# One load cut into 2 and 6 rows in a rotary-embedding kernel that streams 67 MB

## Chip, cores, metric

The kernel runs on one core of one Trainium2 chip. (The experiments used three chips; each was compared with the kernel before in the same rounds on the same chip.) The metric is the time of one execution on the device in microseconds (us). Other times below are counted from the start of the profiled span, which is some 2 us shorter than the device time of the same run.

## The reference, cut to what matters

```
x: (16, 512, 16, 64) float32;  cos, sin: (512, 32) float32
x1, x2 = x[..., :32], x[..., 32:]
first  = x1[..., :16] * cos[..., :16] - x1[..., 16:] * sin[..., :16]
second = x1[..., :16] * sin[..., :16] + x1[..., 16:] * cos[..., :16]
out = concatenate([first, second, x2], axis=-1)
```

Half of each head is rotated, the other half is copied. All of x, 33.6 MB, is read and the same amount is written.

## The kernel before

The kernel cuts x into four tiles of 128 partitions x 16 rows; one row is 16 heads x 64 numbers, 4 KiB. A tile is 8.4 MB, and the kernel keeps room for three, so tile 3 takes the place of tile 0. VectorE rotates a tile in place, in pieces of 8 rows (tile 2's second half in 5 and 3). Loads of x, and all stores but that of tile 2, are issued in program order by SyncE.

```
    def load(t, lo=0, hi=K):
        return nc.sync.dma_start(out=rows(t, lo, hi), in_=xf[t, :, lo * R : hi * R])
    ...
    load(0)
    load(1)
    load(2, 0, KC)                       # KC = 8 rows
    ...                                  # tables of cos and sin
    rotate(0, 0, KC)
    rotate(0, KC, K)
    store(0)
    load(2, KC, K)                       # the load that is changed
    load(3)                              # waits for store(0): same place in memory
    rotate(1, 0, KC)
    rotate(1, KC, K)
    behind_loads = store(1)              # made to wait for `near`
    rotate(2, 0, KC)
    near = rotate(2, KC, KM)             # KM = 13
    rotate(2, KM, K)
    store(2, queue=nc.gpsimd)
    ...
    rotate(3, 0, KC)
    rotate(3, KC, K)
    store(3)
```

Of the kernel before, what the change touches and what calls it, by code (L numbers as in the profile page):

```python
# [1 line left out]

# [4 lines left out]


@with_exitstack
def kernel(  # L10
    ctx: ExitStack,
    tc: tile.TileContext,
    x: bass.AP,
    cos: bass.AP,
    sin: bass.AP,
    out: bass.AP,
):
    nc = tc.nc
    fp32 = mybir.dt.float32
    P = 128  # L20
    B, S, H, D = x.shape
    Q = D // 4
    HF = D // 2



    K = 16
    T = B * S // (P * K)
    PB = S // K
    REP = P // PB  # L30
    R = H * D
    NS = 3
    KC = K // 2
    KM = 13

    xf = x.rearrange("b s h d -> (b s h d)").rearrange("(t p f) -> t p f", t=T, p=P)
    of = out.rearrange("b s h d -> (b s h d)").rearrange("(t p f) -> t p f", t=T, p=P)
    cosf = cos.rearrange("(p k) j -> p (k j)", k=K)
    sinf = sin.rearrange("(p k) j -> p (k j)", k=K)

    const_pool = ctx.enter_context(tc.tile_pool(name="const", bufs=1))
    b_pool = ctx.enter_context(tc.tile_pool(name="bp", bufs=1, space=bass.MemoryType.PSUM))


    ring = const_pool.tile([P, NS, K, H, D], fp32)
    stage = const_pool.tile([P, 2, K, HF], fp32)
    spun = const_pool.tile([P, 2 * K, Q], fp32)
    packed = const_pool.tile([PB, 2 * K, Q], fp32)
    table = const_pool.tile([P, 2, K, 2, Q], fp32)

    def rows(t, lo, hi):
        return ring[:, t % NS, lo:hi].rearrange("p k h d -> p (k h d)")

    def load(t, lo=0, hi=K):
        return nc.sync.dma_start(out=rows(t, lo, hi), in_=xf[t, :, lo * R : hi * R])

    def store(t, lo=0, hi=K, queue=nc.sync):
        return queue.dma_start(out=of[t, :, lo * R : hi * R], in_=rows(t, lo, hi))  # L58


    nc.vector.memset(stage[:, :, :, 0:Q], 0.0)  # L61
    spread = stage.rearrange("(j b) t k i -> j b t (k i)", b=REP)
    nc.gpsimd.dma_start(out=spread[:, 0, 0], in_=cosf)  # L63
    nc.gpsimd.dma_start(out=spread[:, 0, 1], in_=sinf)  # L64
    load(0)
    load(1)
    load(2, 0, KC)




    PQ = PB // REP
    nc.vector.stream_shuffle(  # L73
        out=spun[:],
        in_=stage.rearrange("p t k j -> p (t k) j")[:, :, 0:Q],
        mask=[j % PQ * REP for j in range(PB)],
    )
    for q in reversed(range(REP)):
        n = PQ * (q + 1)
        nc.vector.tensor_copy(out=packed[0:n], in_=spun[q * PB : q * PB + n])  # L80

    for r in range(REP):
        nc.vector.tensor_copy(  # L83
            out=table[r * PB : (r + 1) * PB].rearrange("p t k c j -> p (t k) c j"),
            in_=packed.unsqueeze(2).to_broadcast((PB, 2 * K, 2, Q)),
        )
    C = table[:, 0].rearrange("p k c j -> p k (c j)")
    Sn = table[:, 1].rearrange("p k c j -> p k (c j)")

    def rotate(t, lo, hi):  # L90
        x1 = ring[:, t % NS, lo:hi, :, 0:HF]
        c = C[:, lo:hi].unsqueeze(2).to_broadcast((P, hi - lo, H, HF))
        s = Sn[:, lo:hi].unsqueeze(2).to_broadcast((P, hi - lo, H, HF))
        b_full = b_pool.tile([P, KC, H, HF], fp32, name="b_t")
        b_t = b_full[:, 0 : hi - lo]
        nc.vector.tensor_mul(out=b_t, in0=x1, in1=s)  # L96
        nc.vector.tensor_mul(out=x1, in0=x1, in1=c)  # L97
        nc.vector.tensor_sub(  # L98
            out=x1[:, :, :, 0:Q], in0=x1[:, :, :, 0:Q], in1=b_t[:, :, :, Q:HF]
        )  # L100
        return nc.vector.tensor_add(  # L101
            out=x1[:, :, :, Q:HF], in0=x1[:, :, :, Q:HF], in1=b_t[:, :, :, 0:Q]
        )

    rotate(0, 0, KC)
    rotate(0, KC, K)
    store(0)
    load(2, KC, K)
    load(3)
    rotate(1, 0, KC)  # L110
    rotate(1, KC, K)
    behind_loads = store(1)
    rotate(2, 0, KC)
    near = rotate(2, KC, KM)
    rotate(2, KM, K)
    store(2, queue=nc.gpsimd)

    tc.add_manual_dep(
        behind_loads.ins,
        near.ins.name,  # L120
        mybir.DependencyInfo(mybir.DependencyClass.Sync, mybir.DependencyReason.DATA),
        reason="the store follows the loads at the DMA engines",
# [6 lines that stand above are left out]
# [1 line left out]
_INS = ['x', 'cos', 'sin']  # L130
_OUTS = [((16, 512, 16, 64), 'float32')]


# [23 lines left out]
```

## Time and profile before

| | before |
|---|---|
| time, median of 3 runs | 161.46 us |
| profiled span | 159.5 us |
| VectorE busy | 112.9 us (71%) |
| both DMA queues, share of 16 engines | 98.1% |
| DMA packets | 1360, of them 1152 on the hardware queue |
| last landing of a transfer to the end of the span | 0.886 us |

The lines of the profile are shown in the prediction.

### The profile page before, as it was taken

The numbers are of one execution on the slowest core, as the hardware profiler recorded it, in microseconds if no ns is written. First come the engines' busy times: TensorE is split into PE (matmuls) and PEld (weight loads), VectorE is DVE, ScalarE is ACT, GpSimd is POOL, SyncE is SP. The second block draws the span as 40 slices with busy tenths as digits, with TensorE's granted clock in tenths as the row PEclk, the third lists the DMA queues.
The fourth block names the chain that finished last, engine by engine and source line by source line (L and its number), as shares of the span: only waits on it lengthen the run. The fifth ranks groups of instructions, "written<-read, shape, count | busy, mean of one in ns | idle before, by whom it ended". The sixth has DMA issues, their size and how long they took to land.

```text
span 159.5 us, 115 instructions
## 1 busy us (share of the span) xinstructions
DVE 112.9 (71%) x47; POOL 1.9 (1%) x7
## 2 busy tenths in 40 slices
DVE  1000959999999999999999999999999990000000
POOL 3000000000000000000000000010000000000000
DMA  7969979899699699699996996996996996998966
GB/s 263 542 263 542 444 345 526 362 427 526 271 493 551 263 526 526 263 395 427 493 526 263 526 526 263 526 526 263 526 526 263 526 510 279 526 427 362 526 263 263
DMA packets 1360, 67.24 MB, mean 422 GB/s; under 512 B 176, under 2 KB 176, under 8 KB 208
## 3 DMA queue, kind: packets, MB, share of 16 engines
q1 hardware_dynamic: 1152, 58.72, 85.7%
q0 software_dynamic: 208, 8.52, 12.4%
HBM read 33.69 MB, written 33.55 MB: 422 GB/s over the span
## 4 chain that ended last, share of the span: by engine, by line
DVE 61%; DMA 14%; issue 5%; DVEq 1%
DVE b_t L96 22%; DVE ring L97 22%; DMA ring<-in_x_dram 14%; DVE ring L101 10%; DVE ring L98 7%; DVEq L152 1%; DVEq L96 0%
## 5 line engine op out<-in xcount | busy, mean ns | idle before, releaser
L96 DVE TENSOR_TENSOR b_t<-ring,table 128x4096 f32<-128x4096 f32 (+2 forms) x9 | 35.6, 3959 | 2.1 <-DMA ring<-in_x_dram 1.9
L97 DVE TENSOR_TENSOR ring<-ring,table 128x4096 f32<-128x4096 f32 (+2 forms) x9 | 35.6, 3950 | 0.3
L98 DVE TENSOR_TENSOR ring<-ring,b_t 128x2048 f32<-128x2048 f32 (+2 forms) x9 | 18.4, 2050 | 0.3
L101 DVE TENSOR_TENSOR ring<-ring,b_t 128x2048 f32<-128x2048 f32 (+2 forms) x9 | 18.4, 2043 | 0.0
L73 DVE LOAD_MASK_SELECT spun<-stage x1 | 0.0, 14 | 14.4 <-DMA stage<-in_sin_dram 14.4
L83 DVE COPY table<-packed 32x1024 f32<-32x1024 f32 x4 | 2.7, 684 | 0.1
L58 POOL DMA_DIRECT2D out_dram<-ring x1 | 0.6, 559 | 101.7 <-DVE ring L101 101.7
L80 DVE COPY packed<-spun 32x512 f32<-32x512 f32 (+3 forms) x4 | 1.7, 416 | 0.1
L61 DVE MEMSET stage<- 128x512 f32 x1 | 0.5, 485 | 0.9 <-PEq L141 0.9
L73 DVE STREAM_SHUFFLE spun<-stage 128x512 f32<-128x512 f32 x1 | 0.7, 722 | 0.0
L63 POOL DMA_DIRECT2D stage<-in_cos_dram x1 | 0.6, 642 | 1.3 <-DVE stage L61 1.3
L64 POOL DMA_DIRECT2D stage<-in_sin_dram x1 | 0.5, 532 | 0.0
L141 POOL MEMSET const-bfloat16-1.0<- 128x1 bf16 x1 | 0.1, 101 | 0.0
L141 POOL MEMSET const-float32-0.0<- 128x1 f32 x1 | 0.1, 98 | 0.2 <-issue 0.2
L141 POOL MEMSET const-float32-1.0<- 128x1 f32 x1 | 0.1, 98 | 0.0
L141 POOL MEMSET const-uint8-127<- 128x1 uint8 x1 | 0.1, 98 | 0.0
## 6 DMA issues: line engine op xcount, KB each, us to landing
ring<-in_x_dram SPq DMA_DIRECT2D x2, 4096.0 KB, 40.7
stage<-in_cos_dram POOLq DMA_DIRECT2D x1, 64.0 KB, 8.9
stage<-in_sin_dram POOLq DMA_DIRECT2D x1, 64.0 KB, 13.3
ring<-in_x_dram SPq DMA_DIRECT2D x3, 28.9
out_dram<-ring SPq DMA_DIRECT2D x3, 27.4
out_dram<-ring POOLq DMA_DIRECT2D x1, 39.5
```

The costliest lines, as they stand in the source:

```text
L58: return queue.dma_start(out=of[t, :, lo * R : hi * R], in_=rows(t, lo, hi))
L61: nc.vector.memset(stage[:, :, :, 0:Q], 0.0)
L63: nc.gpsimd.dma_start(out=spread[:, 0, 0], in_=cosf)
L64: nc.gpsimd.dma_start(out=spread[:, 0, 1], in_=sinf)
L73: nc.vector.stream_shuffle(out=spun[:], in_=stage.rearrange("p t k j -> p (t k) j")[:, :, 0:Q], mask=[j % PQ * REP for j in range(PB)],)
L80: nc.vector.tensor_copy(out=packed[0:n], in_=spun[q * PB : q * PB + n])
L83: nc.vector.tensor_copy(out=table[r * PB : (r + 1) * PB].rearrange("p t k c j -> p (t k) c j"), in_=packed.unsqueeze(2).to_broadcast((PB, ...
L96: nc.vector.tensor_mul(out=b_t, in0=x1, in1=s)
L97: nc.vector.tensor_mul(out=x1, in0=x1, in1=c)
L98: nc.vector.tensor_sub(out=x1[:, :, :, 0:Q], in0=x1[:, :, :, 0:Q], in1=b_t[:, :, :, Q:HF])
L101: return nc.vector.tensor_add(out=x1[:, :, :, Q:HF], in0=x1[:, :, :, Q:HF], in1=b_t[:, :, :, 0:Q])
L152: with _tile.TileContext(nc) as tc:
```

## The change

Its likely intent is to have a small first piece of the half tile arrive early, or small packets first where the transfers turn from a store to a load. The whole of it:

```
@@ rotate(0, KC, K); store(0) @@
-    load(2, KC, K)
+    load(2, KC, KC + 2)
+    load(2, KC + 2, K)
     load(3)
```

## The prediction

> **What bounds the kernel now.** I read the page first, then the chain of waits, the SyncE queue's own waits, the timeline, the stretches by window, and last the packet records of the trace (one row per DMA packet: queue, size, start, duration). The page:
>
> ```profile
> span 159.5 us, 115 instructions
> ## 1 busy us (share of the span) xinstructions
> DVE 112.9 (71%) x47; POOL 1.9 (1%) x7
> ...
> ## 3 DMA queue, kind: packets, MB, share of 16 engines
> q1 hardware_dynamic: 1152, 58.72, 85.7%
> q0 software_dynamic: 208, 8.52, 12.4%
> HBM read 33.69 MB, written 33.55 MB: 422 GB/s over the span
> ## 4 chain that ended last, share of the span: by engine, by line
> DVE 61%; DMA 14%; issue 5%; DVEq 1%
> ```
>
> The reader is to see two candidates. The chain names VectorE (61%), but VectorE is busy for 71% of the span, while the packets of the two DMA queues take 85.7 + 12.4 = 98.1% of the time of all 16 engines. The chain is followed through semaphores and so does not see a transfer that queues behind another. The SyncE queue's waits show that queueing:
>
> ```profile
> SPq L152 <- DMA out_dram<-ring: 26.8, 2, 14.4
> SPq L58 <- DMA ring<-in_x_dram: 22.3, 2, 20.8
> SPq L55 <- DMA out_dram<-ring: 21.0, 1, 21.0
> ```
>
> After VectorE's last instruction there are still 26.8 us of waiting for stores. One 8.4 MB tile is 8 packets of 64 KiB on each engine; the packet records give 2418 ns for such a packet and 2414 ns from start to start, so alone it would take 8 x 2.414 = 19.3 us. The other 7 us are a backlog of older stores: VectorE has finished early, and the transfers set the end. The stretches say the same, with the share of the 16 engines next to last and GB/s last:
>
> ```profile
> 2.00:50.00 48.00, 31.94 (x19) 0.87 (x2) 1.00 0.96 415
> 50.00:100.00 50.00, 49.59 (x17) 0.00 (x0) 1.00 1.02 438
> 100.00:158.00 58.00, 30.89 (x12) 0.56 (x1) 1.00 0.98 424
> ```
>
> (A packet is booked where it starts, hence 1.02.) When I string the packets of each engine together, every engine works from 1.7-2.2 us to 158.0-158.2 us, and the largest hole inside that, before the last 0.3 us, is 9 ns. So the kernel is bound by bytes: 67.24 MB through 16 DMA engines that never run dry. Outside this stretch lie 1.7 us until the first packet and about 1.3 us from the last packet to the end.
>
> Two places could open a hole, where loads run out and a store takes over. The timeline:
>
> ```profile
> 49.87 0.35 SPq L58 DMA_DIRECT2D out_dram<-ring  x1
> ...
> 50.26 21.82 SPq L55 DMA_DIRECT2D ring<-in_x_dram  x2
> ...
> 98.86 32.68 SPq L58 DMA_DIRECT2D out_dram<-ring  x2
> ```
>
> The first load was issued at 0.74 and its first packet started at 1.74, so an issue needs 1.0 us to reach the engines. The store of tile 0, issued at 49.87, could start at 50.87; the loads ahead of it drained at about 51.25: 0.4 us to spare. The store of tile 1, issued at 98.86, could start at 99.86; its first packet started at 99.855, as the first engine finished its loads: nothing to spare. The kernel is tuned tightly there.
>
> **What the Trainium skill says.** "Perfetto Trace Analysis", Roofline, says that one core alone is bounded by its 16 DMA engines, about 435 GB/s together. The trace agrees: 65,536 bytes in 2.414 us times 16 is 434 GB/s in steady state. "DMA: Bandwidth & Descriptors", Bandwidth, gives the rule to batch transfers to 1 MiB or more and says that smaller ones pay mostly overhead; one of the two pieces here is just 1 MiB (128 x 8 KiB). But its figure for that size, 341 GB/s, is for a transfer with nothing around it. Here the table loads' 4 KiB packets, interleaved with x's, took 159 ns, and 4/64 of 2418 would be 151: inside a full queue a small packet costs nanoseconds. The same page, Queues, rings and completion order, says that each engine takes its ring's descriptors in order; the trace agrees, since the second half of tile 2 starts only when tile 0's store has ended on its engine. So a piece placed behind that store cannot arrive earlier by being smaller.
>
> **The change part by part.** One SyncE load of rows 8-15 of tile 2 (128 packets of 32 KiB) becomes a load of rows 8-9 (128 of 8 KiB) and one of rows 10-15 (128 of 24 KiB). The order of instructions on VectorE and GpSimd is unchanged; SyncE has one more DMA; the product of rows 8-12 now waits on two load semaphores and not on one. Bytes, tiles and the order of loads and stores stay.
>
> Packets: each engine moves 8 partitions, so it gets 8 more data packets and one more semaphore packet. A split packet's cost can be read from sizes present: a 64 KiB packet takes 2414 ns from start to start, a 32 KiB one 1209.5; two of the latter, 2419, are 4.7 ns more. So 8 x 4.7 + 1 x 6 (the semaphore packet's step) = 44 ns per engine. It lies on the bound, so it counts in full: **+0.04 us**.
>
> Issue: one more SyncE issue of 0.33-0.43 us (the five load issues range from 328 to 433 ns). SyncE next has to issue the load of tile 3, which waits for tile 0's store until 71.8: 21.0 us of waiting by the table above. The extra 0.4 us goes into it: **0**.
>
> Earlier data: rows 8-9 would land about 6 us ahead of the rest (three quarters of 8 x 1.21 = 9.7 us), near 75 us. Their reader needs rows 8-12, so both pieces, and VectorE does not get to it before 90.22, while the whole half landed at 81.34 (last of its 16 semaphore increments). There are 8.9 us of slack already: **0**.
>
> End: the final row of semaphore waits gets one member more, about 0.03 us as a guess from the 21-28 ns of such events in the trace: **+0.03**.
>
> The loads then end 0.04 us later, so the store of tile 1, issued when VectorE says so at 98.86, finds the engines still busy; that gap doesn't open. Sum: +0.07 us on 161.46, thus **161.5 us**.
>
> **Rivals.**
>
> 1. The turn from stores to loads gets cheaper. On 14 of 16 engines the last packet of tile 0's store is not 2418 ns but 2432-3318 ns, and all engines end it between 70.85 and 71.25; this excess averages 0.37 us per engine. Small first packets after a store are perhaps there to fill that. For it: this is the only place in mid-kernel where packets are slow, and it is right before the load that the change cuts. Against it: the slow packet is the store's, which the change leaves alone, and a gain is capped, since the store of tile 1 cannot start before 99.86 and now starts between 99.86 and 100.26; 0.2 us on average would be kept, giving 161.3.
>
> 2. Small packets are slow after all. If an engine can have only few reads in flight, 8 KiB packets could run at half speed: 1 MiB at 434 GB/s is 2.4 us, so up to +2.4 us, 163.9. Against it are the 4 KiB packets at 159 ns; for it, that these alternated with 64 KiB ones and were never eight in a row.
>
> 3. VectorE becomes the bound through a late second piece. It would have to land 8.9 us later than now. The packet sum gives 0.04 us, so I don't believe it.
>
> 4. The extra issue holds up the tile 3 load. At its issue, tile 2's half is still ahead of it (it drains until about 80.8), so even a delay of 8 us would be hidden.
>
> **Range and chances.** The centre is 161.5. The runs before spread from 161.22 to 161.59, and rival 1 takes at most some tenths; rival 2, which I give one chance in ten in some weakened form, puts a tail above. The range is 161.0 to 162.1. 2% is 3.2 us: faster would need fewer bytes or a hole that isn't there (0.01), slower needs more than the worst of rival 2, or one I don't see (0.02).
>
> **What would show it.** Right: 1296 packets on the hardware queue in place of 1152 (128 data and 16 semaphore packets more), still about 98% of the engines; no hole in any engine; the product of rows 8-12 again at about 90.2 with no wait for a load; the store of tile 1 issued at about 98.9. The packets: 8 KiB near 306 ns, 24 KiB near 911 ns (2414 per 64 KiB, plus 5). Wrong: 8 KiB packets of 500 ns or more (rival 2); tile 0's last store packets all at 2418 ns (rival 1); idle time on VectorE ahead of rows 8-12 (rival 3). The number would be wrong without any of these if the chip's runs scatter by more than the three I have.

## The result, and the profile after

In its first six runs the changed kernel took 161.94 us (161.80 to 161.99), the kernel before 161.44 us in its six runs (161.22 to 161.62). The ratio was 1.0029, with a 95% interval of 1.0016 to 1.0042. (A ratio is the mean time of one kernel's fast runs over that of the other's of the same rounds, so it is not quite the ratio of the medians quoted beside it.) That is within 2% and within the stated range, but +0.5 us where the working said +0.07 us.

The first lines are from the page of the changed kernel, packets and queues:

```profile
span 159.9 us, 117 instructions
...
DMA packets 1504, 67.24 MB, mean 421 GB/s; under 512 B 192, under 2 KB 192, under 8 KB 224
## 3 DMA queue, kind: packets, MB, share of 16 engines
q1 hardware_dynamic: 1296, 58.72, 85.7%
q0 software_dynamic: 208, 8.52, 12.3%
...
ring<-in_x_dram SPq DMA_DIRECT2D x1, 3072.0 KB, 30.7
ring<-in_x_dram SPq DMA_DIRECT2D x1, 1024.0 KB, 23.9
```

There are 1296 - 1152 = 144 packets more, as counted, for the same bytes, and the engines are as full as before. The last number of the last two lines is the time from issue to landing: the small piece, issued at 50.43, landed at 74.3 us, the rest, issued at 50.91, at 81.6 us. Next, the timeline near the place that needs these rows (start, duration, engine, line), the kernel before first:

```profile
87.90 2.28 DVE L101 TENSOR_TENSOR ring<-ring,b_t 128x2048 f32<-128x2048 f32 x1
90.22 2.83 DVE L96 TENSOR_TENSOR b_t<-ring,table 128x2560 f32<-128x2560 f32 x1
...
98.86 0.34 SPq L58 DMA_DIRECT2D out_dram<-ring  x1
```

In the changed kernel the same place reads:

```profile
88.07 2.28 DVE L101 TENSOR_TENSOR ring<-ring,b_t 128x2048 f32<-128x2048 f32 x1
90.38 2.83 DVE L96 TENSOR_TENSOR b_t<-ring,table 128x2560 f32<-128x2560 f32 x1
...
99.02 0.34 SPq L58 DMA_DIRECT2D out_dram<-ring  x1
```

No idle time stands behind the product of rows 8-12 (the 128x2560 form), so it waited for no load. The data had come 16 and 9 us earlier; arriving sooner bought nothing. All of VectorE runs 0.16 us later than before, from its first product on, long before the changed load: that is scatter of the start (22.99 us before, 23.16 changed, but 23.15 in experiment 5, which is the kernel before again).

The SyncE queue's waits in the changed kernel, of which those of the kernel before stand in the prediction (total, times, longest):

```profile
SPq L153 <- DMA out_dram<-ring: 27.0, 1, 27.0
SPq L58 <- DMA ring<-in_x_dram: 22.6, 2, 21.0
SPq L55 <- DMA out_dram<-ring: 20.0, 1, 20.0
```

Two things are to be seen. The wait ahead of tile 3's load (last line) shrank from 21.0 to 20.0 us: the extra issue, which took 0.91 us in the trace, was absorbed there. The wait at the kernel's end (first line) was two waits, the longest 14.4 us, and is now one wait of 27.0 us. SyncE closes the kernel by asking for one semaphore after the other, and it now gets stuck earlier in that list. The closing waits of the two kernels, from the trace's instruction records (start in us, duration in ns, semaphores asked for; what follows the first drain is left out):

```
before                                after
131.58     17  110                    131.75     17  110
131.64     28  111, 109               131.80     28  111, 109
131.70     28  112, 100               131.87  26997  112, 100
131.77  12362  113, 103               158.90     28  113, 103
144.16     28  114, 102               158.96     28  114, 102
158.60     28  115, 101               159.02     28  115, 101
158.67      7  drain                  159.09      7  drain
last landing 158.58 (semaphore 115)   last landing 158.84 (semaphore 100)
```

The eight SyncE transfers of the kernel before have eight semaphores, 100 and 109 to 115, and the last store has the last of them, in the last row. The changed kernel has nine; the ninth, again the last store, gets semaphore 100 once more. That one is asked for three rows earlier, so three more rows remain after the last byte has landed. The stretch from the last landing to the end grew from 0.886 to 1.054 us.

The span grew by 0.43 us between these two traces: 0.17 us in that stretch; about 0.05 us for nine more packets per engine; and about 0.2 us at the turn from tile 0's store to tile 2's half, where packets took longer than their usual duration by 0.54 us per engine, against 0.35 us before. The last part is what two traces can't settle.

### The profile page after: what moved, and what is told of

It is laid out like the page before. It is cut to its first block, busy times and chain, and to the rows that moved or that the text cites. A ratio compares the mean times of both kernels' runs of the same rounds, so it can differ in the third digit from the quotient of the medians.

```text
span 159.9 us, 117 instructions
## 1 busy us (share of the span) xinstructions
DVE 112.9 (71%) x47; POOL 1.9 (1%) x7
## 3 DMA queue, kind: packets, MB, share of 16 engines
q1 hardware_dynamic: 1296, 58.72, 85.7%
## 4 chain that ended last, share of the span: by engine, by line
DVE 61%; DMA 14%; issue 5%; DVEq 1%
DVE b_t L96 22%; DVE ring L97 22%; DMA ring<-in_x_dram 14%; DVE ring L101 10%; DVE ring L98 7%; DVEq L153 1%; DVEq L96 0%
```

## The experiments

**Theory.** The change costs two things: three more closing waits after the last landing (0.16 us) and nine more packets per engine (0.05 us). **Rivals:** small packets right after the store make the turn dearer (0.2 us more, so +0.5 us in all); one more SyncE transfer costs 0.5 us wherever it is; small packets are slow everywhere. Eleven kernels ran, all correct. In what follows, the *end stretch* is the time from the last landing to the end, and the *turn excess* is the time by which packets starting between 66 and 84 us exceeded their usual duration, per engine. Both are worked out from the packet and semaphore records of each trace. (If each packet is counted against the median of its size in the same trace, every turn excess comes out up to 0.04 us higher; no comparison changes.)

**1. The changed kernel again** (no edit).

> The changed kernel once more, to see whether the three parts found in its first trace repeat. Between the two first traces the span grew by 0.43 us: 0.17 us from the last landing to the end (0.885 to 1.055), about 0.20 us more excess of packets at the turn from tile 0's store to tile 2's second half (0.35 to 0.54 us per engine), about 0.05 us for nine more packets per engine. Theory (end waits plus turn): +0.5 us against before again, end stretch 1.05 us again, turn excess 0.5 us or more again. Rival (the turn is chance of one trace): the time is again +0.5 us but the turn excess falls anywhere between 0.3 and 0.6, and the rest sits somewhere else.

It took 161.74 us against 161.49 us before, ratio 1.0014 (1.0001 to 1.0027): half of the first difference, so the +0.5 us that both theory and rival expected did not come back. The end stretch was 1.04 us again, the turn excess 0.47 us.

**2. One more small transfer, the half tile whole.** The small load goes into a tile whose data is no longer needed; the definition of `touch` is left out.

```
     load(2, KC, K)
+    touch(0)        # 16 partitions x 512 B of cos into the dead tile `stage`
     load(3)
```

> The kernel before plus one tiny load (16 partitions of 512 B into a tile that is dead by then), issued where the change has its second piece: nine SyncE DMAs, tile 2's half stays whole. Theory: only the end grows, because the last store now signals on the semaphore that the first load had, and the closing waits, taken in fixed order, have three more to go through after it: end stretch 1.05 us, +0.17 us, with 0.03 us for the tiny packets: 161.6, +0.2 us; turn excess 0.35 us as before. Rival (one more SyncE DMA costs 0.5 us wherever it is): +0.5 us. Rival (the size of the pieces is all): +0.0.

It took 161.70 us, ratio 1.0008 (0.9994 to 1.0023). The end stretch was 1.04 us although nothing was split, so it comes from the ninth transfer and not from the pieces. The rival of 0.5 us per transfer falls. (The time alone can't tell +0.2 us from nothing, the end stretch can.) The turn excess was 0.44 us with the half tile whole: the 0.35 us of the first trace was no fixed base.

**3. The same 2-row piece among loads.**

```
-    load(1)
+    load(1, 0, 2)
+    load(1, 2, K)
```

> The kernel before with tile 1's load cut in 2 and 14 rows, and tile 2's half whole: the same 8 KiB packets, but among loads and not after a store. Theory: end +0.17 us, packets +0.05 us, no dearer turn (0.35 us): +0.2 us. Rival (8 KiB packets are slow everywhere): +0.5 us, with 8 KiB packets over 320 ns among the loads. Rival (the turn is chance): as the changed kernel, +0.5 us.

Every one of the 128 packets of 8 KiB took 309 ns, so packets of 8 KiB are not slow by themselves. The end stretch was 1.05 us, the turn excess 0.43 us. But the times were 161.94 to 163.84 us, four of the six over 162.8, ratio 1.0092 (1.0061 to 1.0122). The trace is of the run of 161.94 us and shows nothing of this; experiment 9 takes it up.

**4. The pieces in the other order.**

```
-    load(2, KC, K)
+    load(2, KC, K - 2)
+    load(2, K - 2, K)
```

> The change with the pieces in the other order, 6 rows and then 2: what follows the store is 24 KiB packets, the 8 KiB ones come in the middle of loads. Theory (8 KiB packets right after the store make the turn dearer): end +0.17, packets +0.05, turn near that of before (0.35 to 0.4 us): +0.2 to +0.3 us. Rival (any split of this load costs the same): +0.5 us.

It took 161.78 us, ratio 1.0014 (1.0001 to 1.0028), as the changed kernel did on that chip. Its turn excess was 0.53 us with 24 KiB packets behind the store. This speaks against the 8 KiB packets as the cause, and for scatter.

**5. The kernel before against itself** (no edit).

> The kernel before, against itself: shows how far two sets of runs of one kernel lie apart, and gives a second look at its turn. Theory (the turn's excess is dearer with a split piece): turn excess 0.35 us per engine again, ratio 1.000. Rival (the turn's excess is chance, which the runs so far suggest: 0.35 in the kernel before, 0.54 and 0.47 in the changed one, 0.53 with 6 and 2 rows, 0.44 and 0.43 in the two kernels that leave this load whole): between 0.35 and 0.55 here as well. End stretch 0.885 us in both.

Two sets of runs of one and the same kernel, in the same rounds, gave 161.42 and 161.70 us, ratio 0.998, with an interval (0.9966 to 0.9993) that leaves out 1. So an interval of one call is too narrow to trust at 0.2%: differences of 0.3 us are within what a kernel does against itself. Its turn excess was 0.50 us, where the first trace of it had 0.35; its end stretch was 0.885 us, as the first time.

**6. The changed kernel a third time** (no edit).

> The changed kernel a third time, on the chip of the run above. Theory that remains: end waits +0.16 us and packets +0.05 us, thus +0.2 us, 1.001. Rival: a dearer turn on top, +0.4 us or more, 1.0025 and up, with a turn excess at least 0.1 us over that of the kernel before on this chip.

161.72 us, ratio 1.0004 (0.9991 to 1.0018); turn excess 0.33 us, below both traces of the kernel before; end stretch 1.04 us. A dearer turn at 8 KiB is not to be seen.

**7. Sixteen transfers with the last store in the last row again.** Eight of the small loads are placed so that the last store gets semaphore 115.

```
+    for i in range(6):
+        touch(i)
     store(0)
     load(2, KC, K)
     load(3)
+    touch(6)
+    touch(7)
```

> The kernel before with eight tiny loads of 16 x 512 B, placed so that no issue is late: 16 SyncE DMAs, and the last store gets the eighth semaphore again, the last that the closing waits ask for. Theory (the place of the last store's semaphore in the order of the waits makes the end dearer): end stretch back at 0.885 us although there are more DMAs than in any other run; the tiny packets cost 8 x (23 + 6) ns = 0.23 us per engine, so +0.2 us in all. Rival (the number of DMAs makes the end dearer): end stretch 1.05 us or more, +0.4 us or more.

The time was 161.95 us, ratio 1.0014 (1.0001 to 1.0026), near the 0.23 us expected of the tiny packets (27 ns each in experiment 2). That agreement proves little: it is within what a kernel does against itself, and this trace has 0.24 us per engine of slow packets between 50 and 60 us, where the others have at most 0.07. The end stretch, however, was 0.877 us with twice as many transfers as before. The trace's view of the kernel's last line shows it, for the kernel before, the changed one and this one (duration of the closing waits: least, median, most, in ns):

```profile
L152 SPq EVENT_SEMAPHORE  x8: 17/28/12362, 131.6 to 159.4; - x8
```

```profile
L153 SPq EVENT_SEMAPHORE  x8: 17/28/26997, 131.7 to 159.8; - x8
```

```profile
L163 SPq EVENT_SEMAPHORE  x8: 17/28/12630, 131.8 to 159.9; - x8
```

The number of waits is the same in all. In the first and third the longest is the wait of some 12.5 us for tile 2's store, with the last store's wait behind it. In the second the last store's is taken first and swallows all 27.0 us; the rest of the list comes after. So it is the place in the list that costs, and not the number of transfers.

**8. Eight pieces of one row.**

```
-    load(2, KC, K)
+    for k in range(KC, K):
+        load(2, k, k + 1)
```

> Tile 2's second half in eight loads of one row: 64 packets of 4 KiB per engine right after the store. Packets: 56 more x 4.7 + 7 x 6 ns = 0.31 us; the last store is on the seventh semaphore, so one more closing wait, +0.06 us. Theory (only packets and end): +0.35 to +0.4 us, 161.9. Rival (small packets make the turn dearer): +0.6 us or more, with a turn excess of 0.6 us and more, growing with the number of small packets.

162.60 us, ratio 1.0061 (1.0048 to 1.0073). Here the turn did get dearer: the 64 packets of 4 KiB per engine exceeded their usual 159 ns by 0.62 us in all, and the turn excess was 1.12 us. It is the turn and not a long row of small packets: the 512 of them that started between 76 and 81 us took 159 ns again. Packets (0.3 us), one closing wait (0.05 us) and a turn dearer by some 0.7 us add up to the 1.0 us that the runs show. The windows show it too. For the stretch 72 to 81 us, the DMA share and the GB/s stand last, the kernel before first:

```profile
72.00:81.00 9.00, 8.93 (x4) 0.00 (x0) 1.00 1.21 524
```

```profile
72.00:81.00 9.00, 8.93 (x4) 0.00 (x0) 1.00 1.02 392
```

(Packets are booked where they start, so a stretch with large ones reads high; the packets' own durations carry the verdict.) The dearer turn exists, then, with 4 KiB packets, and not visibly with eight packets of 8 KiB. This run also gives a third point of the closing waits: the last store was on semaphore 114, one row before the last, and the end stretch was 0.936 us. One row more costs 0.936 - 0.886 = 0.050 us; three rows cost (1.044 - 0.886) / 3 = 0.053 us each, with 1.044 the mean over the four traces of the changed kernel.

**9. Tile 1's load in 2 and 14 rows again** (the edit of 3).

> Tile 1's load in 2 and 14 rows once more. Its six runs were 161.94 to 163.84, four of them over 162.8, and its trace was of the fastest. A slower trace is wanted. Theory (the fourth issue at the start delays the small loads of cos and sin, so VectorE starts later and the store of tile 0 comes too late for the engines): in a slow trace VectorE's first product starts over 0.5 us later than 23.0 us and an engine hole opens at about 51 us. Rival (small packets are slow in some runs): no hole, 8 KiB packets over 309 ns. If the trace is again a fast one it stays open.

Two of six runs were long (162.77 and 162.99), the others 161.57 to 161.71; ratio 1.003 (1.0002 to 1.0059). The trace was again of a short run: VectorE started in time, no hole, a turn excess of 0.30 us. So it stays open what six of twelve runs spent 1 to 2 us on.

**10. Tile 1's load in 8 and 8 rows.**

```
-    load(1)
+    load(1, 0, KC)
+    load(1, KC, K)
```

> Tile 1's load in 8 and 8 rows: also nine SyncE DMAs and a fourth issue at the start, but packets of 32 KiB. Theory (the fourth issue at the start): the same spread of 162 to 164. Rival (the 8 KiB packets): steady, and about +0.2 us over the kernel before, with the end stretch at 1.04 us.

Four runs, 161.49 to 161.73 us, ratio 1.0007 (0.9992 to 1.0021), end stretch 1.05 us. None of the four was long. Four runs against a share of one half are a hint and no proof that the fourth issue at the start isn't the cause of the long runs of 3 and 9.

**11. The changed kernel a fourth time** (no edit).

> The changed kernel a fourth time, for the size of the effect. All its runs so far (17) have the mean 161.81, those of the kernel before (31) 161.54: +0.27 us. Theory (0.16 us end waits, 0.05 us packets): +0.2 us, 1.001 with an interval that may include 1; end stretch 1.04 us. Rival (a dearer turn besides): +0.4 us and more.

161.74 us against 161.51, ratio 1.0012 (1.0000 to 1.0024), end stretch 1.04 us, turn excess 0.47 us.

**All together.** The changed kernel's 22 runs have the mean 161.80 us, the 42 of the kernel before 161.54 us: +0.26 us, with a 95% interval of 0.08 us either way if the runs are taken as independent, which experiment 5 says is too kind. The two settled parts give 0.16 + 0.05 = 0.21 us. The traces side by side:

| | end stretch, us | turn excess, us per engine |
|---|---|---|
| half tile whole, 8 transfers: before, before_again | 0.886, 0.885 | 0.35, 0.50 |
| half tile whole, 9 transfers: one_tiny, split_load1, its look, half | 1.04, 1.05, 1.04, 1.05 | 0.44, 0.43, 0.30, 0.37 |
| half tile in 2 and 6: the four traces | 1.05, 1.04, 1.04, 1.04 | 0.54, 0.47, 0.33, 0.47 |
| half tile in 6 and 2 | 1.04 | 0.53 |
| 16 transfers, last store on 115 | 0.877 | 0.23 |
| eight pieces of one row, last store on 114 | 0.936 | 1.12 |

The first column goes by the last store's place in the list: 0.88 to 0.89 us in the last row, 0.94 one row earlier, 1.04 to 1.05 three rows earlier. The second column, the last line apart, shows no such order: the mean is 0.40 us for the six traces of the first two rows and 0.45 us for the four of the changed kernel. Of the excess, the packets behind the store take 0.03 to 0.13 us where they are of 32 KiB, and 0.02 to 0.11 us where they are of 8 KiB. A dearer turn of up to 0.1 us can't be excluded; nothing shows one. That slow packets scatter by this much is seen at the start too, where no edit but those of 3, 9 and 10 touched anything: the packets of the first 10 us exceed their usual durations by 0.56 to 0.79 us per engine in the 13 traces, by 0.77 and 0.62 us in the two of the kernel before. No run points to a kernel faster than that before: whatever was added came on top.

## Why the prediction was right, and where it was off

**The bound.** Right. The engines stayed full, and the order of VectorE and of the transfers stayed. The time moved by 0.2% on the mean of all runs.

**Earlier data, worth 0.** Right: the first piece landed at 74.3 us ("near 75" was said) and its reader started at 90.38 without waiting. The lead over the rest was 7.3 us; three quarters of 9.7 us are 7.3 as well, and not the "about 6" of the text.

**Issue, worth 0.** Right: the wait ahead of tile 3's load shrank from 21.0 to 20.0 us and took up the extra issue, although that took 0.91 us and not the 0.33 to 0.43 us that were read off the issues before it.

**Packets, +0.04 us.** Right in its numbers: by the median, 8 KiB packets took 309 ns and 24 KiB ones 912 ns, and they follow each other after 306 and 908 ns. The two together are 1214 ns, 4.5 ns over the 1209.5 of a 32 KiB packet, where 4.7 was said.

**End, +0.03 us.** This is the term that was mis-sized. The prediction guessed one member more in the final row of waits. It measured 0.16 us, and the row did not get longer: the ninth SyncE transfer took over the first one's semaphore, and so the last store moved from the last row of the closing list to one with three rows behind it, at 0.05 us each. The trace of the kernel before held the eight semaphores and the order in which they are asked for; it was not read for the place of the transfer that lands last.

**Rivals.** The cheaper turn did not come: tile 0's last store packets were no faster than before (0.47 us per engine over 2418 ns, against 0.35; the prediction read the latter as 0.37). The place was well chosen, with the sign reversed: experiment 8 shows that 4 KiB packets there cost 0.6 us. Small packets at half speed did not come at 8 KiB; one of the 128 took 549 ns. Late rows and a held-up load of tile 3 did not come.

**The scatter.** The prediction named it as the way to be wrong without a wrong step. The first comparison, +0.5 us, was about 0.2 us above the mean of all runs; the kernel before, compared with itself, differed by 0.3 us. That the first result, 161.94 us, still lay in the range is in part luck: the upper part of the range was there for slow small packets, which did not come, and not for the end, which did.

## What to carry to other kernels

Here the transfer engines never idled, and cutting a load that was not waited for cost 4.5 ns per packet and gained nothing (with 4 KiB packets right behind a store it cost much more); look up whether its reader waits before asking what an earlier arrival is worth. Count transfers against the semaphores the program has for them: one more than these can put the last store on a semaphore that the closing waits ask for early, and each wait behind it is paid after the last byte. Before explaining a difference of 0.3%, run the old kernel against itself.

## What the Trainium skill lacked or had wrong

- "DMA: Bandwidth & Descriptors", Bandwidth, has no figure for a transfer inside a full queue; its table gives one time per size, for loads issued from GpSimd. Here a piece of 1 MiB among other loads had 128 packets of 8 KiB that all took 309 ns, which is 27 GB/s per engine, as the 64 KiB ones (2418 ns).
- The same page has no cost for the turn from a store to loads on full engines. Here it was 0.23 to 0.54 us per engine, mostly on the store's last packet, and 1.12 us with 64 packets of 4 KiB per engine behind it.
- No page covers the closing waits of a program itself: some 0.05 us for each one after the last landing, and 0.88 to 1.05 us from that landing to the end of the profiled span.
